# A two-layer hybrid trunk: layer A with one decay matrix, plain query products, f32 gates from the normed tiles, and its late modulation in strips of 512

## The chip, the cores and the metric

The kernel runs on one core of one Trainium2 chip. A core has five engines that run side by side, each through its own list of instructions in order: TensorE (PE in the profile; its weight loads, which overlap the matmuls, are PEld), VectorE (DVE), ScalarE (ACT), GpSimd (POOL) and SyncE (SP), which here only issues DMAs. They wait for one another through semaphores. Matmuls write PSUM, which has eight banks of 128 x 512 f32 elements; DVE and ACT read the banks out. The metric is the device time of one execution in microseconds (us).

## The reference

The input x has 1024 tokens of width 1024, in f32. Layer A is a gated DeltaNet, layer B a softmax attention with a forget bias. Only layer A is changed. Its core is this (q and k are normed to length 1 per head, `beta` and `g` come per token and value head from 32 columns of the input projection):

```
qkv, z, b, a = jnp.split(h @ w_in, ...)            # conv of width 4 and SiLU on qkv
beta = sigmoid(b);  g = -exp(A_log) * softplus(a + dt_bias);  g = cumsum(g) in a chunk
decay = exp(where(lower, g[:, None] - g[None, :], -inf))
L = where(strict, (kb @ k.T) * decay, 0);  T = inverse(eye + L)
u = T @ vb;  w = T @ (kb * exp(g));  attn = (q @ k.T) * decay
# chunk after chunk:
v_new = u - w @ S
o = (q * exp(g)) @ S + attn @ v_new
S = S * exp(g_last) + (k * exp(g_last - g)).T @ v_new
```

Before layer A and layer B, x is normed, scaled and shifted by a vector that is made from the condition c and the weights `ada_w` (1024 x 3072 for each layer); after each layer its output is multiplied by a third part of that vector, the gate, and added to x.

## The kernel before

**Tiling.** Layer A runs in two halves h of 512 tokens, each in 8 groups g of one query/key head and two value heads: 16 units i, in four chunks c of 128 tokens (not the reference's 64). For each unit the input projections of k, q, two v and two z are made: per projection 8 steps k of three matmuls of 128 x 512 (`mm3`: the operands are split into a high and a low part in fp32r, products high-high, high-low and low-high). These are the 24 matmuls of a projection tile, named `mm<-ht_h,whi`, `mm<-ht_l,whi` and `mm<-ht_h,wlo` in the profile. All others of layer A are plain f32 matmuls, each of which the trace shows as two entries (the order shows one).

**Who sets the order.** `Flow` is a planner at build time. Generators (`proj_all`, `prepk_all`, `merge_all`, `chain_all`, `finish_all` and others) yield a delay in ns after each piece; `Flow.step` takes the ready one of the first rank. The clock of this plan goes only by a price for each matmul, and the delays, the constants `Y_...`, stand for what DVE, ACT, POOL and the DMAs need. `Flow.bank` gives out PSUM banks, which `Flow.free` gives back after a delay `R_...`. So PE's order is fixed when the program is built, and projections (rank 9) fill it wherever nothing of a better rank is ready. The orders of the other engines come from a scheduler. Where a constant is too small for what really happens, PE stands still in front of the next matmul in its list.

**One unit.** `prepk` (L878) loads a row of decays by DMA, spread over all partitions (`gb`, 512 KB, one buffer); `decay` (L852) masks it on POOL (`affine_select`, L861) and takes eight exponentials on ACT (L873). `to_tokens` (L912) transposes k on PE; ACT squares and copies it out (`sqt`, `ktok`, L919 and L923). The product k k^T times decay gives `lm`; `invert_blocks` (L1064) sends its small blocks through DRAM (`lb`, `lr`, `xi`, `rb`, `rmat`) to invert them on DVE, and `invert_merge` (L1107) joins the blocks by small matmuls. `prep2` (L942) makes a second decay matrix the other way round, with a second load of `gb`, a second mask and eight more exponentials; it also takes exp(`gb`) on ACT (L949), and POOL multiplies the queries by it (`qd`, L950). `prepv` (L926) transposes the two v tiles (`tr<-ident,vt`), ACT copies them out (`vtok`), POOL scales them (L939).

**The chain** (L962), four chunks after one another: `ch<-state,k` (k times state), DVE subtracts it from v (`xp`, L978), `ch<-xp,rmat`, then ACT copies the result out (`vn`, L991) and DVE scales it (`ve`, L992); the output bank gets `co<-state,qd` and `co<-vn,d` for both heads, and `co<-ve,ktok` gives the update that DVE adds to the state (L1011). ACT squares the output and copies it out (L1017, L1020). `finish` (L1031) normalises, transposes, multiplies with the z path and splits the result into `ogh` (ACT) and `ogl` (DVE), both heads in one buffer of each, which two DMAs store.

**Gates** (L660): at the start of each half a projection tile with its own weights, 24 matmuls, then transposes. A unit's `prepk` waits until the gates are in DRAM.

**Late modulation** (`ada_all`, L1195): the rest of `ada_w` in strips of 256 columns, 16 strips of 8 loads of 128 KB, multiplied and added on DVE (L274); PE sums over partitions, and for the four gate strips of each layer DVE copies the row out (`olo`, L301).

After the last projection the output projection `out_proj_a` (L459) fills PE's list, then layer B follows.

## Time and profile before

| what | value |
|---|---|
| median of three timed runs | 2041.61 us (2041.05 to 2041.88) |
| the profiled execution | 2033.73 us |
| its span in the trace | 2032.0 us |
| first projection matmul; last one | at 45.3 us; at 1035.4 us |
| output projection of layer A, until layer B begins | 1036.8 to 1281.1 us |
| DMA share of the span | 47.6% |

The profiled execution is 7.9 us (0.4%) below the median of the timed runs, and 1.7 us of it lie outside the span. A row of a timeline has the start and the length of an instruction or of a run of like ones (`x4`), and in brackets how long its engine stood idle before it and what ended the wait. Matmuls are pipelined: the length contains the time through the array, and what a matmul holds the engine for is read from the distance between two starts. Layer A's projections take the stretch from 45 to 1036 us, which is nearly half of the span.

### The profile page before, as it was taken

Reading aid. Unit: us, or ns where it says so; the run is one execution under the profiler, and the core shown is the slowest. Engines: PE = TensorE matmul, PEld = TensorE weight load, DVE = VectorE, ACT = ScalarE, POOL = GpSimd, SP = SyncE. Lnnn points to the kernel's source line nnn. Section 1 sums busy time; section 2 is a strip of 40 time slices with the busy share of each in tenths; the row PEclk is TensorE's granted clock in tenths of the full one; section 3 lists DMA queues with packets and bytes.
Section 4 is the critical chain, followed back from the end, with each engine's and each line's share of the span. In section 5 each row is a group of like instructions: output and inputs, shape, how many; then the busy total and the mean of one; then the engine's idle time right before and its main releaser. Section 6 shows DMA issues by size and latency. Waiting matters only on the chain. (4 is left out here: it accounts for less than half of the span.)

```text
span 2032.0 us, 36238 instructions
## 1 busy us (share of the span) xinstructions
PE 1846.4 (91%) x12940; PEld 1539.1 (76%) x12940; DVE 1375.5 (68%) x3319; ACT 1035.2 (51%) x2684; POOL 483.0 (24%) x518
## 2 busy tenths in 40 slices
PE   4878899998998989999989789999999999999898
PEld 3766677777776777777777567789889889889676
DVE  5788888787878566766656467456666666656764
ACT  4555466555545445555444344255655655655631
POOL 2140232221213021222101223331231231331222
PEclk6999899999999999999999899999999999999999
DMA  6686676766656455454469988020110220211523
GB/s 248 229 258 226 219 240 208 227 214 223 187 173 172 127 160 160 155 163 134 134 225 311 328 299 285 23 64 22 63 63 17 68 63 16 65 56 42 167 85 96
DMA packets 235781, 315.72 MB, mean 155 GB/s; under 512 B 103176, under 2 KB 155936, under 8 KB 235600
## 3 DMA queue, kind: packets, MB, share of 16 engines
q1 hardware_dynamic: 235600, 313.41, 47.6%
q8 instruction: 102, 1.67, 0.3%
q14 instruction: 79, 0.65, 0.1%
HBM read 231.67 MB, written 81.67 MB: 154 GB/s over the span
## 5 line engine op out<-in xcount | busy, mean ns | idle before, releaser
L129 PE MATMUL mm<-ht_h,whi 128*128 128x512 f32 x784 | 352.4, 450 | 7.2 <-DVE olo L301 5.6
L129 PE MATMUL mm<-ht_l,whi 128*128 128x512 f32 x784 | 317.5, 405 | 3.9 <-DVE ht_l L601 3.9
L129 PE MATMUL mm<-ht_h,wlo 128*128 128x512 f32 x784 | 318.0, 406 | 1.8 <-POOL wlo L328 1.8
L129 PE MATMUL mm<-whi,h_h 128*128 128x384 f32 x512 | 187.0, 365 | 0.9 <-DVE kn L1449 0.9
L129 PEld LDWEIGHTS mm<-ht_h,whi 128*128 128x128 f32 x784 | 154.6, 197 | 40.1 <-DVE olo L301 6.5
L129 PEld LDWEIGHTS mm<-ht_h,wlo 128*128 128x128 f32 x784 | 153.4, 196 | 37.8 <-POOL wlo L328 2.2
L129 PEld LDWEIGHTS mm<-ht_l,whi 128*128 128x128 f32 x784 | 155.0, 198 | 31.0 <-DVE ht_l L601 5.2
L764 DVE SCALAR_TENSOR_TENSOR cv_y<-cv_t,conv_h,cv_y 128x512 f32<-128x512 f32 x192 | 147.6, 769 | 43.0 <-ACT cv_y L756 40.8
L129 PE MATMUL mm<-whi,h_l 128*128 128x384 f32 x512 | 173.0, 338 | 0.0
L129 PE MATMUL mm<-wlo,h_h 128*128 128x384 f32 x512 | 172.7, 337 | 0.0
L1600 DVE TENSOR_TENSOR ptl<-pt,pth 128x512 fp32r<-128x512 f32 x192 | 106.3, 555 | 93.9 <-ACT pth L1599 92.2
L1599 ACT CAST pth<-pt 128x512 fp32r<-128x512 f32 x192 | 91.1, 476 | 140.0 <-PE pt L133 139.2
L1443 POOL TENSOR_TENSOR rs<-ss,mhalf 128x4 f32<-128x4 f32 x64 | 64.5, 1007 | 332.4 <-DVE ss L1441 326.7
L328 DVE TENSOR_TENSOR wlo<-ht_h,whi 128x512 fp32r<-128x512 f32 x124 | 91.1, 775 | 59.7 <-ACT whi L325 54.7
L1564 ACT ACTIVATE lg<-lg,mx 128x896 f32<-128x896 f32 (+7 forms) x128 | 99.5, 777 | 55.4 <-DVE mx L1556 49.7
L325 ACT CAST whi<-ht_h 128x512 fp32r<-128x512 f32 x124 | 70.7, 618 | 95.8 <-PE mm L129 35.3
L129 PE MATMUL mm<-h_h,whi 128*128 128x512 f32 x240 | 99.9, 416 | 0.7 <-DVE wlo L1699 0.3
L129 PEld LDWEIGHTS mm<-whi,h_h 128*128 128x128 f32 x512 | 97.8, 191 | 3.5 <-ACT v L1445 1.2
L129 PEld LDWEIGHTS mm<-wlo,h_h 128*128 128x128 f32 x512 | 97.4, 190 | 2.0
L133 PE MATMUL pt<-ident,lg 128*128 128x128 f32 (+1 forms) x584 | 95.6, 272 | 2.4 <-ACT lg L1564 2.4
L325 ACT CAST whi<-wlo 128x512 fp32r<-128x512 f32 (+1 forms) x108 | 62.5, 625 | 67.2 <-DMA wlo<-in_wa_c_dram 30.9
L129 PEld LDWEIGHTS mm<-whi,h_l 128*128 128x128 f32 x512 | 96.6, 189 | 0.0
(366 smaller groups left out, 4702.0 us busy)
## 6 DMA issues: line engine op xcount, KB each, us to landing
ht_h<-in_wa_o_dram SPq DMA_DIRECT2D x62, 512.0 KB
wc<-whi SPq DMA_DIRECT2D x45, 512.0 KB
wc<-wlo SPq DMA_DIRECT2D x45, 512.0 KB
wlo<-wc SPq DMA_DIRECT2D x45, 512.0 KB
whi<-wc SPq DMA_DIRECT2D x45, 512.0 KB
wlo<-in_wa_c_dram SPq DMA_DIRECT2D x35, 512.0 KB
oraw<-in_ada_w_dram SPq DMA_DIRECT2D x128, 128.0 KB
gb<-g_d SPq DMA_DIRECT2D x32, 512.0 KB
```

The lines of the kernel that those rows point to most:

```text
L129: self.nc.tensor.matmul(out, lhsT, rhs, start=start, stop=stop)
L133: self.nc.tensor.transpose(out, src, ident)
L325: nc.scalar.copy(hi, src)
L328: (lo_eng or nc.gpsimd).tensor_tensor(lo, src, hi.bitcast(F32), op=ALU.subtract)
L764: nc.vector.scalar_tensor_tensor(y, raw[:, j : j + HALF], w[:, j : j + 1], y, op0=ALU.mult, op1=ALU.add)
L1443: nc.gpsimd.tensor_tensor(rs, ss, mhalf[:, 0:4], op=ALU.pow)
L1564: nc.scalar.activation(lg, lg, AF.Exp, scale=-1.0, bias=mx[:, hh : hh + 1], accum_out=sums[:, tt : tt + 1],)
L1599: nc.scalar.copy(ph_[:, cs], pp[:, cs])
L1600: nc.vector.tensor_tensor(pl_[:, cs], pp[:, cs], ph_[:, cs].bitcast(F32), op=ALU.subtract)
```

## The change

**One decay matrix.** `decay` is called once per unit, in the orientation of the old second matrix. `prepk` multiplies k k^T by it into `lm`, which is now the transposed matrix, and `prep2` uses the same matrix for q k^T. `invert_blocks` and `invert_merge` read the transpose: the same number of small matmuls with the operands exchanged. Of scales that sat in other places, `un` and `weg` go; the value tokens are scaled by ACT as it copies them out (`irk`), and POOL's multiplication L939 goes.

**Plain query products.** `qd` and exp(`gb`) go. In the chain one matmul `ch<-state,q` of 256 columns takes the place of the two `co<-state,qd` of 128; ACT scales it by exp(g) (`qe`, two instructions), and DVE adds it to the output (one instruction of 256 columns, in place of ACT's copy). ACT's copy `vn` becomes two instructions with a scale. `co<-ve,ktok` is planned 1000 ns (`Y_C3`) after `co<-vn`.

PE in the first unit of the first half, third chunk, before (co is the output bank, d a decay matrix, ve the scaled new values):

```order
L129 MATMUL mm<-ht_h,wlo 128x512
L129 MATMUL co<-state_139,qd 128x128
L129 MATMUL co<-vn,d_846 128x128
L129 MATMUL co<-state_139,qd 128x128
L129 MATMUL co<-vn,d_846 128x128
L129 MATMUL co<-ve,ktok 128x256
```

and in the changed kernel, at the same chunk:

```order
L136 MATMUL tr<-ident,q 128x128 x4
L132 MATMUL co<-vn,d_656 128x128 x2
L132 MATMUL mm<-ht_h,whi 128x512
L132 MATMUL mm<-ht_l,whi 128x512
L132 MATMUL mm<-ht_h,wlo 128x512
L136 MATMUL tr<-ident,vt 128x128 x4
L132 MATMUL co<-ve,ktok 128x256
```

The matmul that needs `ve` came straight behind the one that needs `vn`; now other work stands between them: six projection matmuls in 38 of the 64 chunks, three in 20, seven in 2 and none in 4.

**Gates in f32.** The gate columns are multiplied in plain f32 with the normed tiles, 32 small matmuls of 32 columns for each half: for the first half inside `start_norm`, ahead of the first projection, for the second in `next_norm`, while the tile is in SBUF. The projection tile of 24 matmuls, its weight load and split go in both halves. PE's list at the start now reads (the first row belongs to the modulation of layer A, the last to the first projection):

```order
L132 MATMUL mm<-cond,zg 128x1 x8
L132 MATMUL tr<-wba,k 128x32 x12
L132 MATMUL tr<-wba,q 128x32 x8
L132 MATMUL tr<-wba,ktok 128x32 x12
L132 MATMUL mm<-ht_h,whi 128x512
```

All 32 gate matmuls stand ahead of the first projection matmul.

**Late modulation.** 8 strips of 512 columns with 64 loads of 256 KB; they begin when the key projection of the sixth unit is made (`AD0`), not after the first gates, and are paced at 3500 ns per load, not 2000. A gate strip's bank is given back after `R_AS` = 2500 ns, not 600.

**Buffers and stores.** Four buffers each for k and q (three and two before), so that the projections may run one unit further ahead; the wait of the q projection for `prep2` goes. `finish` takes one head after the other: `ogt`, `ogh` and `ogl` are half as large, still with one buffer each, and four DMAs of 256 KB store what two of 512 KB did.

ACT's list in the finish of the ninth unit (i = 8), before (`ogh` is the high part of the output, `cv_t` and `cv_y` the convolution's tiles):

```order
L325 CAST ogh<-ogt 128x512
L991 COPY vn<-ch 128x256
L755 COPY cv_t<-mm 128x512
L756 ACTIVATE cv_y<-mm,conv_h 128x512
L325 CAST ogh<-ogt 128x512
```

and in the changed kernel, at the same place:

```order
L328 CAST ogh<-ogt 128x512
L1018 ACTIVATE vn<-ch,wn 128x128 x2
L796 ACTIVATE cv_t<-cv_y 128x512
L328 CAST ogh<-ogt 128x512
L1031 ACTIVATE qe<-ch,g_ex 128x128 x2
L783 COPY cv_t<-mm 128x512
```

The second cast used to write the other half of one buffer; now it writes the buffer that the first one wrote, so it comes after that buffer's store.

The diff, cut to its core (the scales, the order of operands in `invert_merge` and the first norm's buffers are left out):

```diff
-Y_PK = 1200
+Y_PK = 1000
...
-Y_P2 = 4000
+Y_P2 = 3000
...
-Y_C2 = 2000
+Y_C2 = 1700
+Y_C3 = 1000
...
-Y_F1 = 800
-Y_F2 = 2550
+Y_F1 = 900
+Y_F2 = 1600
...
-ADP = 2000
+ADP = 3500
+AD0 = 5
 R_AD = 600
+R_AS = 2500
...
-            flow.free(ps, R_AD)
+            flow.free(ps, R_AS)
...
-        KQ, ZG = 3, 2
+        KQ, ZG = 4, 2
...
+                for t in range(CPH):
+                    mm(
+                        pc[:, t * 32 : t * 32 + 32], xk[:, t * P : (t + 1) * P], wba[:, k],
+                        start=k == 0 and t == 0, stop=k == KT - 1 and t == CPH - 1,
+                    )
...
+                def part(k0):
+                    yield 2000
+                    ps = yield from pst("tr", 2)
+                    for k in range(4):
+                        mm(ps[:, 0:32], hf[0][:, k], wba[:, k0 + k], start=k == 0, stop=k == 3)
...
-            ps = yield from acc_bank()
-            for k in range(KT):
-                mm3(ps, wba_h[:, k], wba_l[:, k], ht_h[:, k], ht_l[:, k], k == 0, k == KT - 1)
...
-                yield from hold(lambda: done["prep2"] >= i - 1)
-                t["q"] = qf = at([P, CPH, P], "q", 2)
+                t["q"] = qf = at([P, CPH, P], "q", KQ)
...
-            _, d1v = yield from decay(t, "d1")
+            t["d2"] = yield from decay(t)
...
-                        d1v[:, u], mq[:, c * P : (c + 1) * P], wn[:, c, j : j + 1], d1v[:, u],
+                        lm[:, u], mq[:, c * P : (c + 1) * P], wn[:, c, j : j + 1], t["d2"][:, u],
...
-            for c in range(CPH):
-                nc.gpsimd.tensor_tensor(vtok[:, c], vtok[:, c], bc(t["un"][:, c], 2, P), op=ALU.mult)
...
-            gb, d2 = yield from decay(t, "d2")
...
-                nc.scalar.activation(gb[:, j], gb[:, j], AF.Exp)
-                nc.gpsimd.tensor_tensor(
-                    qd[:, j], qf, gb[:, j].rearrange("p (c t) -> p c t", t=P), op=ALU.mult
-                )
...
-                nc.scalar.copy(vn, p1[:, 256:512])
+                for j in range(2):
+                    nc.scalar.activation(
+                        vn[:, j * P : (j + 1) * P], p1[:, 256 + j * P : 256 + (j + 1) * P], AF.Copy,
+                        scale=wn[:, c, j : j + 1],
+                    )
...
+                if not first:
+                    mm(p1[:, 0:256], qf[:, c], st)
+                    qe = at([P, 2 * P], "qe", 2)
+                    for j in range(2):
+                        sl = slice(j * P, (j + 1) * P)
+                        nc.scalar.activation(
+                            qe[:, sl], p1[:, sl], AF.Copy, scale=ex[:, 1, c, 2 * g + j : 2 * g + j + 1]
+                        )
...
-                    if not first:
-                        mm(p2[:, sl], qd[:, j, c], st[:, sl], start=True, stop=False)
-                    mm(p2[:, sl], am[:, j, c], vn[:, sl], start=first, stop=True)
+                    mm(p2[:, sl], am[:, j, c], vn[:, sl])
+                yield Y_C3
                 mm(p2[:, 256:512], ktok[:, c], ve.rearrange("p j f -> p (j f)"))
...
-                nc.scalar.copy(og[:, c].rearrange("p j f -> p (j f)"), p2[:, 0:256])
+                    nc.vector.tensor_tensor(oc, p2[:, 0:256], qe, op=ALU.add)
...
-            ogh = at([P, 2, HALF], "ogh", 1, F32R)
-            ogl = at([P, 2, HALF], "ogl", 1, F32R)
-            for j in range(2):
-                split(ogh[:, j], ogl[:, j], ogt[:, j], lo_eng=nc.vector)
+                ogh, ogl = at([P, HALF], "ogh", 1, F32R), at([P, HALF], "ogl", 1, F32R)
+                split(ogh, ogl, ogt, lo_eng=nc.vector)
+                yield Y_F2
+                for v, d in ((ogh, og_d), (ogl, ogl_d)):
+                    nc.sync.dma_start(d[2 * g + j, :, h * HALF : (h + 1) * HALF], v.bitcast(F32))
...
-            yield from hold(lambda: done["gates"] == 1)
+            yield from hold(lambda: done["kp"] >= AD0 + 1)
...
-                for w0 in (0, 256):
-                    yield from ada_strip(
-                        xt_, acc_bank, l, cl + w0, 256, ("oraw", 3), ("ohi", 4), ("olo", 4), 1, ADP
-                    )
+                yield from ada_strip(
+                    al, acc_bank, l, cl, 512, ("nx", 2), ("nh", 2), ("nh", 2), 1, ADP
+                )
```

More of the change, by code (lines that the diff above doesn't have):

```diff
@@ L592, in start_norm @@
             )
+            pc = yield from pst("tr", 2)
             for k in range(KT):
@@ L623, in norm_tile, with xload @@
                 flow.free(ps, R_N)
+                if part is not None:
+                    yield from part(k0)
                 yield 500
+        gts = [{}, {}]
         def next_norm():
             yield from hold(lambda: done["kqv"] >= 2)
[L628 to L635 removed]
+            xts = []
+            def xload(t):
+                tok = CPH * P + t * P
+                xts.append(at([P, D], "nx", 2))
+                if t < 2:
+                    nc.vector.tensor_copy(xts[t][:, 0:KT], ts[0]["gt"]["ngc"][:, 0, 0:KT])
+                nc.sync.dma_start(xts[t], x[tok : tok + P, :])
+            xload(0)
+            yield 6000
+            for t in range(CPH):
+                xt = xts[t]
+                if t < CPH - 1:
+                    xload(t + 1)
+                hf = []
@@ L644, in next_norm @@
+                yield from norm_tile(xt, None, evac, part)
                 yield 3000
-                nc.sync.dma_start(
-                    h1_d[:, :, t * P : (t + 1) * P].rearrange("k p t -> p k t"), hf
-                )
             done["norm"] = 1
+            flow.add(gates(1, gts[1], gin), 1, HC)
         def load_norm():
@@ L658, in load_norm, with gates @@
                     )
[L660 to L678 removed]
+        def gates(h, gt, pv, bank=None):
             tmp = at([P, 6, CPH, 16], "g_tmp")
@@ L685, in gates @@
             nc.scalar.activation(e, e, AF.Exp, scale=-1.0)
-            flow.free(pc, R_N)
+            if bank is not None:
+                flow.free(bank, R_N)
             nc.vector.tensor_scalar(beta, beta, 1.0, None, op0=ALU.add)
@@ L930, in prepv @@
             vtok = at([P, CPH, 2, P], "vtok", 3)
-            for j in range(2):
+            for c0 in range(0, CPH, 2):
                 yield Y_PT
-                yield from to_tokens(vt[:, j], vtok[:, :, j], None)
+                tr = yield from pst("tr", 2)
+                for c in (c0, c0 + 1):
+                    for j in range(2):
+                        o = (2 * (c - c0) + j) * P
+                        tr_(tr[:, o : o + P], vt[:, j, c], ident)
+                for c in (c0, c0 + 1):
+                    o = 2 * (c - c0) * P
+                    nc.scalar.activation(
+                        vtok[:, c].rearrange("p j f -> p (j f)"), tr[:, o : o + 2 * P], AF.Copy,
+                        scale=t["irk"][:, c : c + 1],
+                    )
+                flow.free(tr, R_T)
             done["tr"] += 1
```

193 lines of the change are left out of this document (92 added, 101 removed).

## The prediction

> **What bounds the kernel now.** I read the page first, for the engines, then the busy time by stage, because a mean over two layers hides which of them waits.
>
> ```profile
> PE 1846.4 (91%) x12940; PEld 1539.1 (76%) x12940; DVE 1375.5 (68%) x3319; ACT 1035.2 (51%) x2684; POOL 483.0 (24%) x518
> ...
> 45.00:1036.00 991.00, 888.45 (x7604) 720.67 (x7605) 746.89 (x1887) 526.25 (x1561) 213.07 (x276) 0.95 0.59 187
> 1036.00:1281.00 245.00, 216.43 (x1144) 170.03 (x1133) 149.73 (x260) 104.38 (x218) 54.04 (x36) 0.96 0.86 293
> 1281.00:2032.00 751.00, 721.37 (x4118) 629.74 (x4116) 453.83 (x1136) 388.66 (x858) 202.37 (x178) 0.99 0.19 62
> ```
>
> The columns of the stages are PE, PEld, DVE, ACT and POOL busy, granted clock, DMA share and GB/s. PE bounds all three, and layer A (45 to 1036 us) is where it loses time: it stands idle for 991 - 888.45 = 102.6 us, and the clock of 0.95 costs another 0.05 x 991 = 50 us. Layer B, at 96% and a clock of 0.99, has little to lose and isn't changed. The output projection between them is loaded with DMA (0.86). Its traffic doesn't change, and it starts behind the last projection matmul, so it should move with that matmul as a block.
>
> Next I asked the waits of PE in that stage (total, times, longest). There are 25 rows, the first and the last among these:
>
> ```profile
> PE co L129 <- DVE ve L992: 19.6, 15, 2.3
> PE tr L133 <- ACT vtok L923: 16.0, 5, 7.0
> PE su L129 <- DMA rmat<-rb: 11.1, 2, 9.5
> PE ch L129 <- DVE xp L978: 10.7, 6, 2.6
> PE co L129 <- ACT vn L991: 7.1, 7, 2.8
> PE tr L133 <- ACT ktok L923: 6.0, 1, 6.0
> PE mm L129 <- DVE olo L301: 5.6, 3, 2.4
> PE mm L129 <- DVE ht_l L601: 3.9, 2, 3.4
> ...
> PE tr L129 <- DMA rmat<-rb: 1.5, 1, 1.5
> PE mm L129 <- ACT ht_h L596: 1.4, 1, 1.4
> PE ch L129 <- DVE state L1011: 1.3, 2, 0.8
> ...
> PE su L129 <- ACT qq L1129: 0.2, 1, 0.2
> ```
>
> No engine is slow on the whole; each wait is a place where PE's fixed order allows too little for a result. What one costs beyond itself, the timeline of PE shows at a typical place:
>
> ```profile
> 333.95 0.39 PE L129 MATMUL mm<-ht_l,whi 128*128 128x512 f32 x1
> 334.18 0.40 PE L129 MATMUL mm<-ht_h,wlo 128*128 128x512 f32 x1
> 334.41 0.61 PE L129 MATMUL co<-vn,d 128*128 128x128 f32 x4
> 337.03 0.83 PE L129 MATMUL co<-ve,ktok 128*128 128x256 f32 x2 [2.01 <-DVE ve L992]
> 337.38 0.91 PE L129 MATMUL mm<-ht_h,whi 128*128 128x512 f32 x1
> 338.08 0.63 PE L129 MATMUL mm<-ht_l,whi 128*128 128x512 f32 x1
> 338.51 0.63 PE L129 MATMUL mm<-ht_h,wlo 128*128 128x512 f32 x1
> ...
> 341.77 0.49 PE L129 MATMUL mm<-ht_h,whi 128*128 128x512 f32 x1
> ```
>
> Ahead of the wait projection matmuls start every 0.23 us; behind it every 0.43 us, so the clock is at half until about 341.8. A wait of 2.0 us is followed by 4.4 us at half clock, of which half is lost, another 2.2. I therefore let the 50 us of lost clock go down in the share in which the 102.6 us of waits go down.
>
> The Trainium skill (TensorE: Matmul & The Clock Gate, Part 1) says that the clock falls to half after at least one idle window of about 3.4 us. Here a gap of 2.01 us does it, so the trace is less forgiving than that sentence. What would follow if only long gaps counted is the second rival.
>
> **The change part by part.** The distances between starts give the prices. The first four rows are of PE's timeline, the last two are groups by line (busy us, mean ns, idle before):
>
> ```profile
> 93.74 1.06 PE L129 MATMUL su<-k 128*128 128x128 f32 x8
> 420.58 0.60 PE L129 MATMUL ch<-state,k 128*128 128x256 f32 x2
> 36.95 3.58 PE L129 MATMUL mm<-ones,d 128*128 128x1 f32 x16 [7.95 <-DVE d L574]
> 86.03 0.60 PE L133 MATMUL tr<-ident,g_gc 128*16 128x128 f32 x4
> 154.55 0.38 PE L129 MATMUL su<-rmat,d 32*16 32x16 f32 x4 [9.50 <-DMA rmat<-rb]
> ...
> L129 PE MATMUL su<-k 128*128 128x128 f32 x128 | 17.2, 277 | 2.3 <-ACT pp L1153 2.3
> L129 PE MATMUL ch<-state,k 128*128 128x256 f32 x112 | 34.4, 389 | 2.0 <-DVE state L1011 1.3 <-DVE ln_ss L308 0.6
> ```
>
> *Work of PE.* Eight entries of 128 columns take 1.06 us, less 0.28 for the last one's way through the array, so 0.11 each; an entry of 256 columns takes 0.60 - 0.39 = 0.21. The 112 `co<-state,qd` (two entries each) held PE for 112 x 0.22 = 25 us; 56 `ch<-state,q` hold it for 56 x 0.42 = 23.5. That is **-1.5**: the plain query product saves weight loads, not columns. A gate tile of 24 matmuls costs 24 x 0.23 = 5.5. No row has an f32 matmul of 32 columns; the nearest is the f32 matmul of one column, 8 in 3.58 us at half clock, so 0.43, and 0.21 at full clock. Thirty-two cost 6.8 to 13.7 us. In the second half they run in the stream at full clock: 6.8 - 5.5 = **+1.3**. At the start PE is at half clock (the 0.43) and waits anyway (3.9 + 1.4 us for `ht_l` and `ht_h`): between 6.8 - 5.5 - 5.3 = -4 and 13.7 - 5.5 = +8, and I take **+3**.
>
> *The wait for `ve`* (19.6 in 15 pieces, 1.3 on average, 2.3 at most). With 6 projection matmuls in between in 38 of 64 chunks (1.4 us), and 3 in 20 (0.7), most pieces vanish; I leave 4: **-15.6**. The longer chain costs nothing while projections fill the list. What is late next is the state: behind `co<-ve` the order now has a median of 2.1 us of work ahead of `ch<-state,k` (2.8 before, by counting matmuls at these prices), and DVE adds the output in the same place. The state wait was 1.3 us; **+2**.
>
> *The waits behind exponentials.* The longest `vtok` wait reads so on POOL, ACT and PE:
>
> ```profile
> 620.65 1.18 POOL L861 TENSOR_SCALAR_AFFINE_SELECT d<-gb 128x1024 f32<-128x1024 f32 x1 [3.50 <-DMA gb<-g_d]
> 621.86 0.98 ACT L873 ACTIVATE d<-d,g_ngc 128x128 f32<-128x128 f32 x3 [1.46 <-POOL d L861]
> 625.25 0.56 ACT L923 COPY vtok<-tr 128x512 f32<-128x512 f32 x1
> 625.87 1.12 PE L133 MATMUL tr<-ident,vt 128*128 128x128 f32 x4 [7.01 <-ACT vtok L923]
> ```
>
> POOL waits for a second load of the one `gb` buffer, ACT waits in order for POOL, and the copy that frees PE's bank stands behind. With one load per unit half of these places go: of 16.0 + 6.0 I take **-11**, between 0 and -22.
>
> ```profile
> L873 ACT ACTIVATE d<-d,g_gc 128x128 f32<-128x128 f32 x128 | 39.2, 389 | 22.6 <-POOL d L861 13.7 <-POOL cv_t L759 8.9
> L274 DVE SCALAR_TENSOR_TENSOR ohi<-oraw,cond,ohi 128x256 f32<-128x256 f32 x112 | 65.5, 584 | 14.2 <-DMA oraw<-in_ada_w_dram 13.4
> L991 ACT COPY vn<-ch 128x256 f32<-128x256 f32 x64 | 24.0, 374 | 36.8 <-PE ch L129 36.6
> L1017 ACT ACTIVATE sqt<-co 128x128 bf16<-128x128 f32 x128 | 35.2, 275 | 98.8 <-DVE state L1011 63.8 <-DVE xi L1090 10.7 <-PE mm L129 8.3
> ```
>
> The instructions that go are hidden themselves: ACT's 128 exponentials (39 us of 526 busy, in 991) and POOL's masks and multiplications (POOL is busy for 213). They count for nothing, and so do the exchanged operands of the inversion, the same number of matmuls. `vn` in two parts costs ACT 2 x 0.28 to 2 x 0.39 in place of 0.37, at most 0.4 us more, against the new 0.43 of `ch<-state,q` ahead of the reader: 0, cover gone +0.4 x 64 = 26 at the far end.
>
> *The first inversion* (9.5 of the 11.1 + 1.5 for `rmat`). From the transposes of the gates to the landing pass 154.55 - 86.03 = 68.5 us. In the new order 81 projection matmuls stand ahead of those transposes, not 138, and 300 ahead of the first inversion, not 291. The first projection comes at about 56 (45 plus the gate matmuls, 6.8 to 13.7); then the transposes come at 75 and the blocks at 144; PE gets there at 56 + 300 x 0.23 + 8 of transposes and products, plus some 9 us of other waits and half clock, so at 142. A wait of 2 to 4 stays: **-6**.
>
> *The late modulation.* On DVE 112 instructions of 256 columns become 56 of 512, each at 0.58 to 1.17 us: 0 to 33 us less, and they begin later, when the first units are through. DVE isn't the bound; I take 0, and a few us off `xp` at the low end. SP issues half as many loads at a slower pace, which no wait of PE names. The gate strips' wait (5.6) does count: half as many, and a bank planned 1.9 us later against a longest wait of 2.4: **-4.6**. The fourth buffer of k and q and the removed wait for `prep2` only let projections move earlier in the list; the order above counts that.
>
> *The stores of `finish`.* SP issues them in order, and ACT's second cast now waits for the first's store; behind it in ACT's list stand `qe` and the convolution's copy, which frees a projection bank, and DVE's `ogl` waits in the same way. The nearest row is another store of 512 KB that ACT had to wait for:
>
> ```profile
> ACT nh L307 <- DMA h_d<-nh: 5.8, 2, 5.6
> ```
>
> So a landing takes up to 5.6 us, perhaps half of it for 256 KB. The cast's own instructions and the next head's transposes cover 2 to 3 us, and the projection banks more. Between 0 and 16 x 3 = 48 on PE; I take 0.5 per unit, **+8**. By the Trainium skill (DMA: Bandwidth & Descriptors, Anatomy of one DMA) a DMA costs about 2 us plus bytes at 436 GB/s; an estimate from that is 2.6 us for 256 KB, though its fit is for another issuing engine, and the term would be 0.
>
> *Sum.* Waits that go: 15.6 + 11 + 6 + 4.6 = 37.2 of 102.6. Clock with them: 50 x 37.2 / 102.6 = **-18**. All: -37.2 - 18 - 1.5 + 1.3 + 3 + 2 + 8 = **-42.4**. From the profiled execution's 2033.7 that leads to 1991; the median of the timed runs lies 7.9 higher, so **1999 us**.
>
> **The rivals.**
>
> *Slower: the stores of `finish` hold ACT.* Without this term the change gains 50.4. Each us that PE loses per unit costs 16 x 1.49 with its clock (152.6 / 102.6 = 1.49), so the gain is gone from 2.1 us per unit on. At 3 us: 16 x 3 x 1.49 - 50.4 = +21, so 2063. For it: the 5.6 us above, and one buffer. Against it: two projection banks, and only half the bytes. 12%.
>
> *Only long gaps bring half clock.* Then the clock comes back at the three longest waits alone (9.5, 7.0, 6.0), 2.2 us each, 6.6 in place of 18: 2010. The place at 337 us speaks against it. 13%.
>
> *The waits only change their names.* PE's list runs ahead until the next result is late: DVE is busy for 747 of 991 us and gets another 56 additions, and `xp` and `vn` (10.7 and 7.1) keep their places. Then only a few us are left, 2039. 10%. That a part does nothing at all is not likely, since the order shows each.
>
> **How the numbers follow.** The forecast of 1999 us has 65%. The low end takes the four groups in full: 19.6 + 22 + 5.6 + 12.6 = 59.8, clock 29, and 2.8 for the gates and products, but nothing for the state and stores: -86, so 1956. The high end lies just past no change, 2045. A measurement tells 0.2%, about 4 us, from no change. Faster by more: 65% + 13%, less 1% for the forecast's far end, 77%; within 0.2%: 10%; slower: 13%.
>
> **What would show it.** Right: in the stage from the first to the last projection the idle time falls to about 75 us and the clock rises to about 0.97; the `ve` row falls under 5 us; the last projection starts near 993; the later stages keep their lengths. Wrong: a new row of tens of us at `ogh`, `ogl` or the projection banks, or as many us in `xp`, `vn` and `state` as have left `ve`. If the idle time falls and the clock stays at 0.95, the share of the clock is the step that failed.

## The result and the profile after

The changed kernel takes 2127.95 us (median of 4 runs, 2124.67 to 2139.52). The kernel before, run beside it, takes 2041.74 us (2041.05 to 2042.71). The ratio is 1.0432, with a 95% interval of 1.0392 to 1.0472: **slower by 4.3%**, where the prediction said 1999 us and put its upper end at 2045. The profiled execution took 2126.55 us.

The page gives the engines' busy time, and among its costliest groups one line (busy us, mean ns, idle time before it and what ended that):

```profile
PE 1884.8 (89%) x12892; PEld 1565.0 (74%) x12892; DVE 1339.5 (63%) x3321; ACT 1036.4 (49%) x2672; POOL 366.4 (17%) x402
...
L132 PE MATMUL ch<-state,q 128*128 128x256 f32 x112 | 44.9, 487 | 102.7 <-DVE ve L1022 102.7
```

VectorE, GpSimd and TensorE's instruction count all went down as the diff promises. Yet TensorE stood idle for 102.7 us in front of one kind of instruction, the new plain query product, and always for `ve`. The stages, in the columns of the prediction (stretch, its length, the five engines' busy time, clock, DMA share, GB/s):

```profile
45.00:63.00 18.00, 13.91 (x65) 13.78 (x65) 7.72 (x12) 8.06 (x12) 0.00 (x0) 0.50 0.00 0
63.00:1123.00 1060.00, 909.06 (x7686) 730.73 (x7686) 706.62 (x1877) 520.30 (x1542) 99.76 (x162) 0.94 0.52 166
1123.00:1377.00 254.00, 218.69 (x932) 170.78 (x932) 146.25 (x258) 103.19 (x212) 53.05 (x36) 0.93 0.83 283
1377.00:2124.00 747.00, 722.93 (x4118) 631.27 (x4116) 453.16 (x1136) 388.90 (x858) 203.31 (x178) 0.99 0.19 62
```

The first projection now starts at 63 us and not at 45. The projections end 87 us later than before (1123 against 1036). The output projection is 9 us longer, and layer B 4 us shorter: together the 92 us between the two spans. In the projection stage TensorE is idle for 1060 - 909.06 = 150.9 us.

TensorE's waits there (total, times, longest), the first rows and three of the smaller ones:

```profile
PE ch L132 <- DVE ve L1022: 95.2, 51, 6.7
PE ch L132 <- DVE xp L1004: 8.6, 6, 4.3
PE ch L132 <- DVE state L1048: 7.1, 7, 1.7
PE su L132 <- ACT rmat L1202: 6.0, 4, 2.7
PE tr L136 <- ACT vtok L964: 6.0, 2, 4.9
PE ch L132 <- DVE state L1046: 4.8, 2, 4.1
...
PE co L132 <- ACT vn L1018: 0.7, 1, 0.7
PE tr L132 <- ACT ktok L947: 0.7, 1, 0.7
PE ch L132 <- ACT ogh L328: 0.5, 1, 0.5
```

Read against the table of before, nearly every row that the prediction wanted smaller is smaller: `co<-ve` (19.6), `rmat<-rb` (11.1) and `olo` (5.6) have gone, and `vtok` with `ktok` fell from 22.0 to 6.7. One row, which did not exist, is larger than all that went. All 56 query products (recorded as 112) waited, 1.17 us at the least, 1.8 on average (102.7 / 56), 6.7 at the most. What the wait consists of, the timeline of TensorE, ScalarE and VectorE shows at its shortest, which 21 of them have:

```profile
630.07 0.60 PE L132 MATMUL ch<-xp,rmat 128*128 128x128 f32 x4
...
630.71 0.63 ACT L1018 ACTIVATE vn<-ch,wn 128x128 f32<-128x128 f32 x2 [2.39 <-PE ch L132]
631.37 0.42 DVE L1022 TENSOR_TENSOR ve<-ch,wex 128x256 f32<-128x256 f32 x1 [0.59 <-ACT vn L1018]
631.85 0.70 PE L132 MATMUL ch<-state,q 128*128 128x256 f32 x2 [1.18 <-DVE ve L1022]
632.20 0.58 PE L132 MATMUL mm<-ht_h,whi 128*128 128x512 f32 x1
```

TensorE makes `ch`; ScalarE reads it (`vn`), then VectorE reads it (`ve`, which starts when `vn` has ended, though it doesn't use `vn`), and only then does TensorE write the query product into the other half of the same bank. The product needs neither `vn` nor `ve`. But it is written behind them in the program and touches their bank, so it waits for both (the experiments below move it and give it another bank). It stands in TensorE's list directly behind `ch<-xp`, so nothing covers the wait, and the projections behind it in the list wait too.

The Trainium skill (PSUM — Partial Sum Buffer, PSUM bank collisions raise a hardware error) says that two engines may not use one bank and quadrant at once, whatever columns they touch, reads against reads included, and that software therefore guards by bank and quadrant and not by address. The trace agrees with the order that follows from it: the three instructions above never overlap. What happens where they do, no run here shows.

### The profile page after: what moved, and what is told of

Its sections match the earlier page's. It is cut to its first block, busy times and chain, and to the rows that moved or that the text cites. A ratio compares the mean times of both kernels' runs of the same rounds, so it can differ in the third digit from the quotient of the medians.

```text
span 2124.4 us, 35838 instructions
## 1 busy us (share of the span) xinstructions
PE 1884.8 (89%) x12892; PEld 1565.0 (74%) x12892; DVE 1339.5 (63%) x3321; ACT 1036.4 (49%) x2672; POOL 366.4 (17%) x402
## 5 line engine op out<-in xcount | busy, mean ns | idle before, releaser
L132 PE MATMUL mm<-ht_h,wlo 128*128 128x512 f32 x768 | 312.5, 407 | 0.0
L132 PE MATMUL mm<-ht_l,whi 128*128 128x512 f32 x768 | 311.3, 405 | 0.0
L132 PE MATMUL ch<-state,q 128*128 128x256 f32 x112 | 44.9, 487 | 102.7 <-DVE ve L1022 102.7
L132 PEld LDWEIGHTS ch<-state,q 128*128 128x128 f32 x112 | 18.6, 208 | 113.6 <-DVE ve L1022 113.6
L328 ACT CAST whi<-wlo 128x512 fp32r<-128x512 f32 x106 | 60.3, 616 | 77.0 <-PE mm L132 47.2
```

Of the source, the lines that this page charges most:

```text
L132: self.nc.tensor.matmul(out, lhsT, rhs, start=start, stop=stop)
L328: nc.scalar.copy(hi, src)
```

## The experiments

The main theory (A): the place of that one line costs the whole loss. Its rivals: VectorE and ScalarE are late in general (B), or the start, the stores or the strips lose the time (C). Ratios stand against the kernel before, run on the same chip; in brackets is the 95% interval.

**1. The product ahead of the readers.** One line moves; TensorE's list stays the same, instruction by instruction, without the wait.

```diff
+                if not first:
+                    mm(p1[:, 0:256], qf[:, c], st)
                 vn = at([P, 2 * P], "vn", 2)
                 ve = at([P, 2, P], "ve", 2)
...
                 if not first:
-                    mm(p1[:, 0:256], qf[:, c], st)
                     qe = at([P, 2 * P], "qe", 2)
```

> The changed kernel with one line moved: the plain query product into columns 0:256 of the chain's bank is written ahead of the two `vn` copies and of `ve`, which read columns 256:512 of the same bank. TensorE's list of instructions is the same, in the same order; only the wait for `ve` on the query product is gone. Theory A (the new row 'PE ch <- DVE ve: 95.2' is the whole loss, because the product stands in TensorE's list at a place where the readers of its bank are never done): the 102.7 us row falls under 5 us, nothing of its size takes its place, and the time falls by 90 to 120 us, to 2010 to 2040, of which up to 20 us by a better clock. Rival B (VectorE and ScalarE are late in general, and the wait only names the last of them): some 70 us come back as waits of `co<-vn`, `xp` and `state`, and the time stays above 2090. Rival C (the time is lost at the start and in the finish stores): above 2100.

Measured: 1980.23 us, ratio 0.9697 (0.9678 to 0.9716), 148 us below the changed kernel and more than A said. The stretch ahead of the projections and their stage, and then a chunk in the timeline of TensorE, ScalarE and VectorE:

```profile
45.00:62.40 17.40, 13.91 (x65) 13.78 (x65) 7.47 (x12) 7.47 (x11) 0.00 (x0) 0.50 0.00 0
62.40:978.00 915.60, 863.33 (x7682) 703.00 (x7683) 701.16 (x1876) 513.93 (x1538) 99.70 (x162) 0.98 0.61 192
```

```profile
202.13 0.60 PE L132 MATMUL ch<-xp,rmat 128*128 128x128 f32 x4
...
202.57 0.60 PE L132 MATMUL ch<-state,q 128*128 128x256 f32 x2
...
203.20 0.63 ACT L1020 ACTIVATE vn<-ch,wn 128x128 f32<-128x128 f32 x2 [2.08 <-PE ch L132]
203.86 0.42 DVE L1024 TENSOR_TENSOR ve<-ch,wex 128x256 f32<-128x256 f32 x1 [0.36 <-ACT vn L1020]
```

Idle time fell from 150.9 to 52.3 us (-98.6), and busy time for the same matmuls from 909.06 to 863.33 (-45.7), at a clock of 0.98 instead of 0.94. The bank's order is still there: now the reader `vn` waits until the product is through. But that wait is ScalarE's and not TensorE's. B and C fall.

**2. The product behind the planned pause.** The wait stays, the place changes:

```diff
+                yield Y_C1
                 if not first:
                     mm(p1[:, 0:256], qf[:, c], st)
...
                 flow.free(p1, R_C + 1000)
-                yield Y_C1
```

> The changed kernel with the query product, its two scalings and the return of the bank moved behind the pause of 1.7 us that follows `ve`, so that the projections which fill that pause stand ahead of it in TensorE's list; the wait for `ve` stays on it. Theory A (the place is what costs, not the wait): the row of the query product falls from 102.7 to under 15 us, the chain's bank comes free a little later (some 0.5 us in each of 112 steps, hidden), and the time is 2015 to 2050. Rival B (engines late in general): above 2090. If the first experiment helps and this one doesn't, it is not the place but the later return of the bank that decides.

Measured: 2010.68 us, ratio 0.9848 (0.9817 to 0.9879). The row of the product by line:

```profile
L132 PE MATMUL ch<-state,q 128*128 128x256 f32 x112 | 38.9, 431 | 23.8 <-DVE ve L1022 23.2
```

From 102.7 to 23.8 us, with projections ahead of it. That is more than the 15 us expected, and the median is 4 us below the 2015 to 2050 that A named. The direction is A's, the sizes are not; B (above 2090) falls again.

**3. The product in a bank of its own**, at its old place behind the readers:

```diff
-                    mm(p1[:, 0:256], qf[:, c], st)
+                    pq_ = yield from pst("tr", 2)
+                    mm(pq_[:, 0:256], qf[:, c], st)
```

> The changed kernel with the plain query product at its place behind the readers, but into a bank of its own from the pair that the transposes use, instead of into the chain's bank. Theory A (it is the dependence on the readers of the chain's bank): the wait for `ve` goes; waits for a free bank of that pair take its place in part, since transposes hold it; the row comes to 15 to 50 us and the time to 2000 to 2060. Rival (the product at this place is costly whatever bank it goes to, since it is issued before its inputs or its engine are ready): the row stays above 80 us and the time above 2100.

Measured: 1971.66 us, ratio 0.9654 (0.9630 to 0.9677), the fastest kernel of the study. The row by line, and a chunk:

```profile
L132 PE MATMUL tr<-state,q 128*128 128x256 f32 x112 | 34.0, 386 | 0.9 <-DVE nh L668 0.9
```

```profile
215.11 0.60 PE L132 MATMUL ch<-xp,rmat 128*128 128x128 f32 x4
215.55 0.60 PE L132 MATMUL tr<-state,q 128*128 128x256 f32 x2
215.75 0.62 ACT L1018 ACTIVATE vn<-ch,wn 128x128 f32<-128x128 f32 x2 [2.19 <-PE ch L132]
```

Waits for a free bank came to 0.9 us in its place, against 15 to 50 expected, and `vn` now runs while TensorE makes the product. So the wait comes from the shared bank, and not from the place as such. The time, too, is below the 2000 to 2060 that A named. (Its last projection starts within 1 us of that of the first experiment, so the further 8.6 us by the medians arise behind it, where the two kernels differ little; I don't claim them for this edit.)

**4. The plain product alone, on the kernel before.** Two decay matrices, gates, strips and stores stay; queries get a third buffer.

```diff
-                nc.scalar.activation(gb[:, j], gb[:, j], AF.Exp)
-                nc.gpsimd.tensor_tensor(
-                    qd[:, j], qf, gb[:, j].rearrange("p (c t) -> p c t", t=P), op=ALU.mult
-                )
...
+                if not first:
+                    mm(p1[:, 0:256], qf[:, c], st)
...
-                    if not first:
-                        mm(p2[:, sl], qd[:, j, c], st[:, sl], start=True, stop=False)
...
+                    nc.vector.tensor_tensor(oc, p2[:, 0:256], qe, op=ALU.add)
```

> The kernel before with the plain query product alone (product from the raw queries, at the place where the change puts it, two scalings on ScalarE, the sum on VectorE; the exponential and GpSimd's product for the modulated queries are gone; three buffers of queries in place of two). Two decay matrices, the gates by projection, the strips and the finish stores are as before. Theory A: the loss is in this part and shows without the others: a row of 80 to 110 us on the query product, and a time of 2110 to 2150. Rival C (start, finish stores or strips): no row above 20 us there, and a time of 2030 to 2060.

Measured: 2158.63 us, ratio 1.0567 (1.0552 to 1.0583), 9 us beyond A's range. The row:

```profile
L129 PE MATMUL ch<-state,q 128*128 128x256 f32 x112 | 47.1, 508 | 109.3 <-DVE ve L985 109.3
```

So the loss needs no other part of the change.

**5. The same, with the product ahead of the readers** (the line moved as in experiment 1):

> The kernel before with the plain query product alone, as in the run that measured 2158.6 us, but with the product written ahead of the readers of its bank. Theory A (only the place of that one line cost the 115 us): the row of 98.4 us goes, with it the low clock, and the time is 2005 to 2040, that is no slower than the kernel before, since the exponentials and GpSimd's products for the modulated queries are gone. Rival (the plain product costs in itself, by the sum on VectorE and the scalings on ScalarE, and the other parts of the change pay for that): 2040 to 2070.

Measured: 2038.88 us, ratio 0.9993 (0.9975 to 1.0011). No difference from before can be told, so the line's place is worth 120 us there. What the plain product is worth in itself lies between -5 and +2 us (the interval times 2042). The prediction's -1.5 fits that, but is too small to be shown by it.

**6. The gates behind the first projections**, on the changed kernel:

```diff
-            flow.add(gates(0, gts[0], pc[:, 0 : CPH * 32].rearrange("p (c n) -> p c n", n=32), pc), 1, HC)
+            flow.add(gates0(xsT), 1, HC)
...
+        def gates0(xsT):
+            yield 4000
+            pc = yield from pst("tr", 2)
+            for k in range(KT):
+                for t in range(CPH):
+                    mm(
+                        pc[:, t * 32 : t * 32 + 32], xsT[k][:, t * P : (t + 1) * P], wba[:, k],
+                        start=k == 0 and t == 0, stop=k == KT - 1 and t == CPH - 1,
+                    )
```

> The changed kernel with the 32 thin matmuls of the first half's gates taken out of the start and put into a generator of their own that begins 4 us behind the first projections. Theory A: the first projection starts near 47 us instead of 63 us, the matmuls then run at the full clock (32 in some 5 us instead of 15), and the time falls by 8 to 16 us, to 2112 to 2120; the row of the query product stays near 100 us. Rival: the first chains can't begin earlier for want of the gates, or the clock is as low without the thin matmuls, and the time stays within 4 us of the changed kernel's 2128.

Measured: 2136.32 us, ratio 1.0451 (1.0429 to 1.0472), no better than the changed kernel: theory A was wrong here, and the rival's 4 us around 2128 are missed by 4 us, though the two intervals overlap. The projections do start at 44.6 us. But the clock shows something I had not looked for, by stretch of time (the gates' 32 matmuls, recorded as 64, lie between 57.6 and 67.1):

```profile
57.60:60.20 2.60, 2.60 (x25) 2.56 (x23) 1.65 (x3) 2.21 (x4) 0.30 (x1) 1.00 0.47 129
60.20:62.00 1.80, 1.80 (x18) 1.80 (x18) 1.73 (x3) 0.00 (x0) 0.00 (x0) 1.00 0.98 401
62.00:67.10 5.10, 5.10 (x26) 5.10 (x26) 0.86 (x2) 0.63 (x1) 0.10 (x1) 0.50 0.25 101
67.10:72.30 5.20, 5.20 (x13) 4.13 (x14) 4.38 (x18) 0.62 (x3) 0.00 (x0) 0.50 0.00 0
```

TensorE is never idle, and yet the clock halves 4.4 us into the run of 32-column matmuls and comes back only after another 5 us of projections.

**7 and 8. Late gates on top of experiment 1, in one piece and spread out** (in the second, `yield 1500` follows each k step):

> The changed kernel with the query product ahead of the readers and, besides, the first half's gates behind the first projections in one piece. In the run with the gates alone the 64 thin matmul records began at a granted clock of 1.00 and fell to 0.50 some 4 us later with no gap between them, and the projections behind them needed 5 us to regain the full clock. Theory T (a stretch of thin matmuls counts as idle for the clock): the same drop here, and a time within 8 us of the 1980.2 us without the move (1972 to 1986). Rival (the start's 17 us are won once the chain no longer waits): 1958 to 1968.

> As the run with both edits, but each of the eight k steps of the gates (8 thin matmul records, some 0.9 us) is followed by a planned pause of 1.5 us, which projections of 128x512 fill. Theory T: the clock stays at 1.00 through the gates, the thin matmuls take some 7 us in all, the second group of 96 projections starts near 78 us instead of 88, and the time is 1960 to 1975. Rival (thin matmuls have nothing to do with it, the first projections start slow in any case): same drop, and a time within 4 us of the run in one piece.

Measured: 1980.88 us, ratio 0.9719 (0.9695 to 0.9742), in one piece, and 1981.70 us, 0.9721 (0.9702 to 0.9741), spread. In one piece the clock falls again, 5.3 us into the run of thin matmuls. Spread out, it stays up; the stretch that holds the gates reads

```profile
58.30:80.00 21.70, 21.70 (x129) 19.03 (x128) 12.04 (x17) 8.45 (x15) 1.11 (x5) 1.00 0.58 215
```

So theory T is right about the clock in both, and about the time in one piece (1972 to 1986). Spread out it expected 1960 to 1975, and the time doesn't move. The first instruction of the first chain, in experiment 1, in the piece and spread (min/median/max ns, then first and last start):

```profile
L132 PE MATMUL ch<-vtok,rmat x4: 270/274/275, 180.9 to 181.2; 128*128 128x128 f32 x4
```

```profile
L132 PE MATMUL ch<-vtok,rmat x4: 270/274/275, 185.4 to 185.8; 128*128 128x128 f32 x4
```

```profile
L132 PE MATMUL ch<-vtok,rmat x4: 270/274/275, 184.0 to 184.3; 128*128 128x128 f32 x4
```

It starts between 181 and 185 us whether the projections begin at 62 or at 45 (and at 181 in the kernel before). So the lead of 17 us is gone by then. Something between the gates and that chain must set its start; what it is, these runs do not show.

**9. Three buffers of keys and queries** (`KQ` 3, not 4), on top of experiment 1:

> The changed kernel with the query product ahead of the readers, and three buffers of keys and of queries in place of four: sizes one part of the change alone. The sum of the prediction gave no time to this part. If that is right: 1974 to 1988. If the fourth buffer lets the projections run ahead of the chain (its worth can't be seen in the trace of before, where a plain query product didn't hold the queries): new waits for `k` or `q` and 1990 to 2020.

Measured: 1986.63 us, ratio 0.9754 (0.9728 to 0.9780). That lies in the range expected for a buffer that is worth nothing (1974 to 1988). Beside experiment 1 it is 6 us slower by the medians and 12 by the ratios (0.0057 x 2042), and the intervals just part: the fourth buffer, which I had given nothing, is probably worth a little.

**10. Two buffers for the stores of `finish`**, on top of experiment 9:

```diff
-                ogh, ogl = at([P, HALF], "ogh", 1, F32R), at([P, HALF], "ogl", 1, F32R)
+                ogh, ogl = at([P, HALF], "ogh", 2, F32R), at([P, HALF], "ogl", 2, F32R)
```

> The changed kernel with the query product ahead of the readers and three buffers of keys and queries (1986.6 us), and besides two buffers each for the high and the low part that `finish` stores, so that ScalarE's cast doesn't wait for the store of the half before (15.5 us of waits there, 6.7 us on VectorE). Sizes the prediction's term for those stores, +8 us (0 to 48). If the term holds: 1976 to 1981. If ScalarE's wait is hidden behind TensorE's projections: 1983 to 1990, with both waits gone from the trace.

Measured: 1979.81 us, ratio 0.9684 (0.9654 to 0.9715). Beside experiment 9 that is 7 us by the medians and 14 by the ratios (0.0070 x 2042), so the stores cost about what the term of +8 had. The waits of 15.5 us on ScalarE and 6.7 us on VectorE are gone from the trace.

**11. The strips early again**, as in the kernel before, on top of experiment 9:

```diff
-            yield from hold(lambda: done["kp"] >= AD0 + 1)
+            yield from hold(lambda: done["gates"] == 1)
...
-                yield from ada_strip(
-                    al, acc_bank, l, cl, 512, ("nx", 2), ("nh", 2), ("nh", 2), 1, ADP
-                )
+                for w0 in (0, 256):
+                    yield from ada_strip(
+                        xt_, acc_bank, l, cl + w0, 256, ("oraw", 3), ("ohi", 4), ("olo", 4), 1, ADP
+                    )
```

> The changed kernel with the query product ahead of the readers and three buffers of keys and queries (1986.6 us), and besides the modulation strips as in the kernel before: 256 columns, early, in the output projection's buffers, with the earlier pace. Sizes the part 'late strips of 512' alone. The prediction gave this part -4.6 us: then 1988 to 1995 here, and the `olo` row of before (5.6 us) is back. Rival (the part is worth nothing or costs, since the strips now share buffers with the norm of the second half): 1978 to 1986.

Measured: 2034.64 us, ratio 0.9966 (0.9949 to 0.9983): **48 us slower** than experiment 9 by the medians, 43 by the ratios (0.0212 x 2042). That is about ten times the term, and outside both ranges (1988 to 1995, or 1978 to 1986). By stretch, experiment 9 first, then this one:

```profile
45.00:200.00 155.00, 143.00 (x1110) 119.98 (x1111) 109.21 (x287) 84.71 (x216) 18.29 (x34) 0.89 0.62 205
200.00:400.00 200.00, 185.47 (x1585) 150.17 (x1583) 161.88 (x450) 123.50 (x368) 23.44 (x44) 0.99 0.65 213
400.00:1000.00 600.00, 562.95 (x5132) 456.98 (x5132) 443.88 (x1171) 321.05 (x988) 60.32 (x85) 0.98 0.57 176
```

```profile
45.00:200.00 155.00, 129.33 (x797) 107.09 (x796) 115.98 (x304) 72.55 (x172) 13.60 (x31) 0.84 0.69 225
200.00:400.00 200.00, 175.09 (x1612) 140.88 (x1613) 154.33 (x438) 108.98 (x328) 23.23 (x36) 0.92 0.59 190
400.00:1000.00 600.00, 566.72 (x4988) 461.90 (x4987) 426.26 (x1157) 325.08 (x996) 60.72 (x94) 0.97 0.54 168
```

All of it is lost ahead of 400 us: 24 us more idle (355 - 304.4 against 355 - 328.5), and a clock of 0.84 and 0.92 in place of 0.89 and 0.99, which is another 0.05 x 155 + 0.07 x 200 = 22. Behind that the two run alike: the 870th of the 2304 projection matmuls starts at 399 us in experiment 9 and 52 us later here, the last one 43 us later (987 and 1030 us).

**12. Late strips alone, on the kernel before** (only their beginning moves):

```diff
-            yield from hold(lambda: done["gates"] == 1)
+            yield from hold(lambda: done["kp"] >= 6)
```

> The kernel before with one edit: the modulation strips begin when the sixth group's keys are projected, not when the first half's gates are done; width, buffers and pace stay. In the changed kernel with early strips (2034.6 us against 1986.6 us without) the stretch from 62 to 200 us ran at a clock of 0.88 in place of 0.94, and the second inversion's rows left some 40 us later. Theory S (the 64 first-layer and layer-B weight loads and their products on VectorE compete with the preparation of the first chains, and nothing that TensorE waits for names them): the wait of 11 us for `rmat<-rb` goes, the second chain starts 10 us earlier or more, and the time falls by 20 to 45 us, to 1997 to 2022. Rival (the early strips cost only beside the changed kernel's buffers and second-half norm): 2034 to 2046.

Measured: 2058.04 us, ratio 1.0092 (1.0062 to 1.0121): slower by 18 us, outside S's range (1997 to 2022) and the rival's (2034 to 2046). Theory S falls as a general claim. The kernel before, then this one:

```profile
45.00:200.00 155.00, 127.01 (x981) 100.12 (x982) 127.34 (x308) 85.15 (x215) 32.95 (x46) 0.89 0.71 231
200.00:400.00 200.00, 178.16 (x1532) 143.37 (x1531) 171.15 (x429) 118.13 (x361) 50.10 (x64) 0.94 0.69 218
400.00:1000.00 600.00, 550.94 (x4823) 450.83 (x4822) 423.57 (x1082) 307.35 (x941) 124.69 (x161) 0.96 0.54 170
```

```profile
45.00:200.00 155.00, 133.42 (x1027) 107.03 (x1028) 112.37 (x267) 89.58 (x226) 25.92 (x46) 0.89 0.62 207
200.00:400.00 200.00, 174.29 (x1501) 142.01 (x1501) 154.62 (x396) 118.98 (x358) 49.44 (x67) 0.94 0.63 205
400.00:1000.00 600.00, 544.09 (x4639) 440.00 (x4638) 431.26 (x1131) 295.03 (x902) 116.47 (x154) 0.94 0.57 178
```

The start does gain (6 us more of TensorE's time used before 200 us), and the second unit's chain starts 10 us earlier (211 us against 221), as S said. But where the strips now lie (their loads leave between 354 and 871 us), from 400 us on, TensorE is busy less and at a lower clock. The 700th of the 2352 projection matmuls starts 12 us earlier than before, the 1000th 2 us earlier and the last one 16 us later. What the late strips are worth depends on the other parts: 48 us one way beside them, 18 the other way alone. Width, buffers and pace differ between the two experiments as well. Which of these decides, and which resource the early strips take from the first chains, stays open.

## Why the prediction was wrong

**The step that failed** is the first of its part by part, "Work of PE": 56 `ch<-state,q` were priced as columns on TensorE, -1.5 us, and given no wait. With the wait gone, nothing contradicts the price of the columns (experiment 5). But a matmul that goes into a bank which others are reading has a place in the program relative to those readers. In the change it comes after them: 102.7 us of waiting, in 56 pieces of 1.8 on average. The prediction even set the product's 0.43 us, as work of TensorE "ahead of the reader", against the longer `vn` of ScalarE. In the changed kernel it cannot begin until `vn` and `ve` are through, so it covers nothing; only in experiment 3 does it run beside `vn`. The list of TensorE alone does not show the difference, since both kernels have the same one; what each instruction waits for does.

**The clock** was right on average. The prediction let each us of waiting cost 152.6 / 102.6 = 1.49. From the changed kernel to experiment 1 it was (98.6 + 45.7) / 98.6 = 1.46. That is why a wait of 103 us cost 148. The reading of the single place was not quite right. There the granted clock, by windows cut where it changes (columns as above), reads

```profile
334.05:337.46 3.41, 1.40 (x10) 1.09 (x8) 3.41 (x11) 0.00 (x0) 0.84 (x1) 1.00 0.92 302
337.46:340.87 3.41, 3.41 (x12) 2.66 (x11) 3.41 (x10) 3.12 (x10) 2.30 (x2) 0.50 0.96 356
340.87:344.29 3.42, 3.35 (x21) 2.63 (x21) 3.42 (x10) 3.39 (x13) 0.00 (x0) 1.00 1.03 293
```

so the half clock lasted 3.41 us and not 4.4. In the projection stage of all three kernels (before, changed, experiment 1) each stretch of half clock is a whole multiple of 3.41 us, on a grid that is fixed within the run, and it goes with how long TensorE stood idle in the window of 3.41 us ahead of it. Of 785 such windows at full clock, none of the 696 with less than 1.2 us of idle time was followed by half clock, 15 of the 55 with 1.2 to 1.92 us were, and all 34 with more. The changed kernel has 24 stretches of half clock, 122.9 us in all, and experiment 1 has 8, 34.1 us. Half of the difference, 44, is the 45.7 above. So 1.46 is a mean over waits of very different cost: one of 1.17 us alone cost no clock. The rule of the Trainium skill (TensorE: Matmul & The Clock Gate, Part 1) that an idle window of some 3.4 us is needed would have left most of that out: only three of the 56 waits are as long. The trace agrees with the window's length, but a window that was idle for 1.9 of its 3.41 us was enough.

**The waits that should go went.** The forecast in those places (15.6 + 11 + 6 + 4.6) is met or passed in the trace of experiment 1. With the product ahead of its readers the kernel lands at 1980 us, inside the prediction's range and 19 below its value, at an idle time of 52.3 + 3.5 = 56 us where 75 was named, and a clock of 0.98 where 0.97 was.

**The state** is later than I allowed: 7.1 + 4.8 = 11.9 us against 1.3, not 1.3 + 2 (3.6 + 2.8 in experiment 1).

**The start** was wrong twice, and without consequence. I put the first projection at 56 us; it came at 63, since the gates ran at half clock throughout and the waits for the normed tiles (3.2 us for ScalarE's `k`, 1.9 for VectorE's) were added, not covered. And the +3 us that I charged are 0, because the first chain starts no later than before (181 us in both the kernel before and experiment 1), and late gates don't bring it forward (experiments 7 and 8).

**The stores of `finish`** were right in size (+8 forecast, 7 to 14 measured), and as a rival (up to 3 us per unit) wrong: TensorE's own row for `ogh` is 0.5 us. The landing behind it ranges widely: the stores of `ogh` landed after 2.0 us (median) in the changed kernel and after 3.6 in experiment 9. So neither the 2.8 that I took, half of 5.6, nor the estimate of 2.6 from the Trainium skill (DMA: Bandwidth & Descriptors, Anatomy of one DMA) can be called the better one.

**The strips** are the other mis-sized term: -4.6, read from the one row that named them (`olo`), against 48 measured beside the other parts. Read the other way, experiment 11 is the change with its product ahead of the readers and three buffers, but with the strips early, and it stands only 7 us below the kernel before (0.0034 x 2042). The prediction's sum without the strips is some 36 (42.4 less 4.6 and 2.2 of clock). So the waits that went were worth their forecast only together with the late strips. A transfer or a VectorE product that is never what TensorE waits for *last* may still delay what it does wait for; that this is the way here is argued and not shown. That the sum came out near experiment 1 is therefore partly luck: its largest single part was not in it, and it is not additive.

**The forecast of rivals** missed the mechanism. "The waits only change their names" came nearest, but it let the new waits be as long as the old ones. It had no case in which a new wait at a new place exceeds all of those.

## What to carry to other kernels

When a matmul is added to a bank that is in use, list that bank's readers in program order and ask what stands in TensorE's queue between the last of them and the new matmul: if nothing, the readers' full time is a TensorE stall in each iteration. Emit the matmul ahead of the readers, or give it another bank; both cured it here, with the order of TensorE's work unchanged in the first case. Price such stalls with the clock that goes with them (1.46 times here, as a mean of many), and don't size a moved load by the row that carries its name.

## What the runs showed of the hardware

- Half clock came and went by windows of 3.41 us, and went with the idle time of TensorE, in one piece or several, within the window before. Counted from the first to the last projection in all 14 traces, half clock followed all 145 full-clock windows with more than 1.92 us of idle time, 75 of the 222 with 1.2 to 1.92, and 5 of the 3243 with less. Two of these 5 are the windows full of thin matmuls of the next point.
- A run of thin matmuls halves the clock, though TensorE never idles: 32-column f32 matmuls began at 1.00 and fell to 0.50 after 4.4 us (experiment 6) and 5.3 us (experiment 7), each time at the end of the first of these windows that they filled. The same matmuls in groups of four with 128x512 projections in between kept 1.00 (experiment 8). The Trainium skill (TensorE: Matmul & The Clock Gate, Part 1) has the window as one of activity and ties the half clock to idle ones; here it came with a window in which TensorE had work throughout. Whether the narrow columns do it or the weight load that each of them brings, no run here separates.
- VectorE and ScalarE, both only reading one bank, ran one after the other in the chunk shown above (630.71 to 631.34, then 631.37), though neither needs the other's result. VectorE's wait there ended with ScalarE's `vn`, so this is an order that the program holds; no run here shows the chip without it.
